# One copy of the bias table, four product banks, and a lane for the compression in a two-layer hybrid-attention trunk

## The chip, the cores and the metric

The kernel runs on one NeuronCore of a Trainium2 chip. The metric is the time of one execution on the device in microseconds, the median of several runs; lower is better. A profile of one execution shows, for each engine, which instruction ran when. TensorE (PE) multiplies, with its weight loads shown apart (PEld); VectorE (DVE) and ScalarE (ACT) work element by element; GpSimd (POOL) does little here but issues some of the DMAs; SyncE (SP) issues the others.

## The reference

A trunk of two layers works on a sequence of 256 rows of width 1024 in float32. Each layer has a gated FFN, three kinds of attention side by side whose outputs are gated and merged, a second gated FFN, and a gated addition of a per-layer embedding:

```python
for i in range(DEPTH):
    h = h + 0.5 * swiglu(rms_norm(h, norm_g[i, 0]), ffn1_wi[i], ffn1_wo[i])
    n = rms_norm(h, norm_g[i, 1])
    (aq, ak, av, bq, bkc, ..., ga, gb, gc) = split_cols(n @ w_in[i], IN_SPLITS)
    ya = diff_attention(aq, ak, av, bias_a, lam, ...)         # A: two softmaxes, subtracted
    yb = nsa_attention(bq, compress(bkc), compress(bvc), bks, bvs, bkw, bvw, ...)  # B
    yc = swa_sink_attention(cq, ck, cv, bias_c, sinks[i])     # C: window 128, with a sink
    merged = sigmoid(ga) * (ya @ w_branch[i, 0]) + sigmoid(gb) * (yb @ w_branch[i, 1]) \
           + sigmoid(gc) * (yc @ w_branch[i, 2])
    h = h + merged @ w_out[i]
    h = h + 0.5 * swiglu(rms_norm(h, norm_g[i, 2]), ffn2_wi[i], ffn2_wo[i])
    h = h + sigmoid(rms_norm(h, norm_g[i, 3]) @ w_ple_gate[i]) * (p[i] @ w_ple[i])
return rms_norm(h, final_norm)
```

All three attentions add to their scores a bias that depends on the head (20 of them) and on the distance between query and key alone. In attention B the keys and values are also compressed: blocks of 32 rows, one every 16, pass through a small network with GELU (`w1`, then `w2`) to 15 compressed keys and values, to which every query attends as well.

## The kernel before

**Products.** The 256 rows are two tiles of 128, called t = 0 and 1. Each product has a weight stream: pieces of 128 x 1024 floats (512 KB) come in by DMA to one of four `raw` buffers (L257, issued on SP), and each is split into a rounded part `wh` (ScalarE, L213) and a remainder `wl` (VectorE, L208). `mul3` (L219) makes one full-precision product out of three fast matmuls, L220 to L222. `product` (L290) walks over the k chunks of tile 0, then of tile 1, and calls `done(t, ps)` when a tile's sum is complete. `done` reads the PSUM bank and frees it. Products take their bank from `mm_bank` (L191), which has two; two more banks (tag "s") hold attention's scores, three (tag "tp") transposes, one (tag "y") attention outputs.

**Order.** The program is written in one order, and a scheduler places each engine's instructions by when their inputs are ready, earlier-written ones first. After that each engine runs its list strictly in order. A DMA's wait holds back what is behind it on its queue.

**FFN.** `ffn` (L437) runs 11 products `ff` of 512 columns (gate and up halves of 256), whose `done` is `gated` (L452): ScalarE's `act` (L458), then VectorE's multiplication (L459). Their results are transposed by DMA (`turn_by_dma`, L420). The two output products are `fo`.

**Attention beside products.** Attention A, C and B are generators. `Flow` (L153) holds one of them at a time and advances it by `pace` steps on each k step of a product (`tick`); `join` (L171) runs the rest of it in one go. L955 to L977 give the order: A runs beside the products Ck, Cq and Bk and is joined; C runs beside Bv, Bq and branch 0 and is joined; B runs beside the product of the compression, branch 2 and the gates of branch 1, and is joined before the last two branch products (L941).

**Compression.** `compress` (L685) multiplies with `w1` (L701 to L707), copies the sum (L709), folds it (`gl`, L712), goes through GELU, multiplies with `w2` for keys (`kc`) and, group by group, for values (`vc`, 16 rows, L735 to L740), all in one stretch. `attend_cmp` (L761) scores against the compressed keys and turns the eight heads' probabilities by eight transposes of 16 columns each (`pct`, L787), into `pcT` with 16 rows. The last step of each group and tile of B multiplies `pcT` with `vc` (L843) and gathers the output (L748).

**Bias.** `setup` (L1041), run between products of the first FFN, makes a table of 20 heads x 384 distances, writes it to DRAM (`table`, 30 KB, L1061), and has POOL copy it 128 times into `rev` (3840 KB, L1062). A band of four heads for 128 queries x 256 keys is then one DMA that steps one element back per partition (`rev_band`, L1033): two for `cbias` in `setup`, and five in each layer's attention. `softmax` (L523) adds the band to the scores and takes the minimum in one VectorE instruction (L529).

Of the kernel before, what the change touches and what calls it, by code (L numbers as in the profile page):

```python
# [26 lines left out]
NB = 20  # L27
# [6 lines left out]
PACE_A, PACE_B, PACE_C = 0.75, 0.7, 0.6  # L34
# [101 lines left out]
def _constants():  # L136
    u = np.arange(REV)
    dist = 255 - u
# [10 lines left out]
    return {"onehot": onehot, "dead": dead, "cmask": cmask, "ident": np.eye(128, dtype=np.float32),  # L149
# [3 lines left out]
class Flow:  # L153


    def __init__(self):
        self.side, self.pace, self.due = None, 0.0, 0.0

    def start(self, side, pace):
        self.side, self.pace, self.due = side, pace, 0.0  # L160

    def tick(self):
        if self.side is not None:
            self.due += self.pace
            while self.due >= 1.0:
                self.due -= 1.0
                if next(self.side, self) is self:
                    self.side = None
                    return

    def join(self):  # L171
        if self.side is not None:
            for _ in self.side:
                pass
            self.side = None
# [3 lines left out]
def trunk(ctx: ExitStack, tc: tile.TileContext, a: dict, out: bass.AP, index: list):  # L179
# [11 lines left out]
    def mm_bank(name):  # L191
        return bank("mm", 2, name)

# [96 lines left out]
    def product(lhs, nk, done, name, w, skew=SKEW):  # L290

        def run():
            ps = [None] * NT
            for step in range(nk + skew):
                for t, k in ((0, step), (1, step - skew)):
                    if 0 <= k < nk:
                        wh, wl = w(k)
                        if k == 0:
                            ps[t] = mm_bank(f"{name}{t}")
                        xh, xl = lhs(t, k)  # L300
                        mul3(ps[t][:, :w.width], xh, xl, wh, wl, k == 0, k == nk - 1)
                        if k == nk - 1:
                            done(t, ps[t])
# [184 lines left out]
    def attention(i, norm, after):  # L488
# [3 lines left out]
        def begin():  # L492
            nonlocal pool
            pool = phase("attn")
            for t in range(NT):
                merged[t] = pool.tile([128, D], F32, name=f"merged{t}")
# [58 lines left out]
        def band(first):  # L555
            b = pool.tile([128, 4, 256], F32, tag="band", bufs=2, name="band")
            rev_band(b, first)
# [23 lines left out]
        def attend_a():  # L581
            bnd = band(0)

            def first(u):
# [6 lines left out]
                for st in softmax([p[:, j, :nk] for j in range(4)], [s[j // 2][:, j % 2, :nk] for j in range(4)],  # L591
                                  [bnd[:, 2 * m + j % 2, 256 - nk:] for j in range(4)]):
# [90 lines left out]
        kc, vc = [None], [None]  # L683

        def compress():  # L685
# [22 lines left out]
            c_sb = stage()  # L708
            nc.vector.tensor_copy(c_sb[:64], c_ps[:64])  # L709
            g_ps = tp_bank("gl")[:, :128]  # L710
            for k in range(4):
                nc.tensor.matmul(g_ps[:, 32 * k:32 * k + 32], c_sb[:64, 128 * k:128 * k + 128], fold, start=True, stop=True)  # L712
# [3 lines left out]
            nc.vector.tensor_tensor(gl, gl, g_ps, op=ALU.mult)  # L716
            nc.scalar.activation(gl, gl, AF.Tanh, scale=math.sqrt(2.0 / math.pi))
            nc.vector.tensor_scalar(gl, gl, 0.5, 0.5, op0=ALU.mult, op1=ALU.add)
            nc.vector.tensor_tensor(gl, gl, g_ps, op=ALU.mult)
            hid = pool.tile([128, 2, 128], F32R, name="hid")  # L720
            split(hid[:, 0], hid[:, 1], gl)
            w2h, w2l = w2(0)
# [10 lines left out]
            split(kt[:, 0], kt[:, 1], kbd)  # L733
            v_ps = tp_bank("vc")
# [4 lines left out]
            vc[0] = pool.tile([16, 2, 128], F32R, name="vc")  # L739
            values(vc[0], v_ps[:16, :128], None)  # L740
# [20 lines left out]
        def attend_cmp(t):  # L761
# [20 lines left out]
            for g in range(2):  # L782
                ps = tp_bank("pct")
                for par in range(2):
                    for m in range(2):
                        j = 2 * par + m
                        nc.tensor.transpose(ps[:16, 128 * j:128 * j + 128], p[:, 4 * g + 2 * m + par, :], ident)  # L787
                T = pool.tile([16, 2, 512], F32R, tag="pcT", bufs=2, name="pcT")
                split(T[:, 0], T[:, 1], ps[:16])
                pcT[t, g] = T  # L790
# [381 lines left out]
```

## Time and profile before

| | us |
|---|---|
| median of 3 runs | 1372.09 (1371.64 to 1373.06) |
| the profiled execution | 1372.78 |
| its span, first to last instruction | 1371.0 |
| TensorE busy | 1341.5 |
| VectorE busy | 944.7 |
| ScalarE busy | 779.4 |
| chain that ended last: TensorE / DMA / VectorE / ScalarE | 88% / 5% / 3% / 2% |

The busy time of TensorE is modelled from the ends of pipelined matmuls, which overlap, so counts of matmuls in a window tell more than its busy share. "Granted clock" is the share of TensorE's full 2.4 GHz that it was given; 0.50 is 1.2 GHz.

### The profile page before, as it was taken

Reading aid. Unit: us, or ns where it says so; the run is one execution under the profiler, and the core shown is the slowest. Engines: PE = TensorE matmul, PEld = TensorE weight load, DVE = VectorE, ACT = ScalarE, POOL = GpSimd, SP = SyncE. Lnnn points to the kernel's source line nnn. Section 1 sums busy time; section 2 is a strip of 40 time slices with the busy share of each in tenths; the row PEclk is TensorE's granted clock in tenths of the full one; section 3 lists DMA queues with packets and bytes.
Section 4 is the critical chain, followed back from the end, with each engine's and each line's share of the span. In section 5 each row is a group of like instructions: output and inputs, shape, how many; then the busy total and the mean of one; then the engine's idle time right before and its main releaser. Section 6 shows DMA issues by size and latency. Waiting matters only on the chain.

```text
span 1371.0 us, 18293 instructions
## 1 busy us (share of the span) xinstructions
PE 1341.5 (98%) x6454; PEld 1098.2 (80%) x6454; DVE 944.7 (69%) x1779; ACT 779.4 (57%) x1378; POOL 19.0 (1%) x37
## 2 busy tenths in 40 slices
PE   8988999999999999999999999999999999999997
PEld 6766888887787788888888888888887778888886
DVE  7546656777886766766677665667697776776665
ACT  7435445668766455545665444566785656455454
POOL 0000000000000000000000000000000000000000
PEclk9999999999999999999999999999999999999999
DMA  8797757444653467775657885754547435777662
GB/s 306 199 265 227 216 177 237 142 152 156 215 175 109 153 189 213 215 210 192 203 189 219 223 226 171 235 170 137 162 151 232 127 122 168 216 222 218 194 202 84
DMA packets 121993, 261.07 MB, mean 190 GB/s; under 512 B 56816, under 2 KB 62372, under 8 KB 121774
## 3 DMA queue, kind: packets, MB, share of 16 engines
q1 hardware_dynamic: 121006, 254.34, 60.3%
q0 software_dynamic: 464, 5.01, 1.2%
q8 instruction: 50, 0.82, 0.2%
q10 hardware_dynamic: 432, 0.56, 0.1%
q14 instruction: 41, 0.34, 0.1%
HBM read 247.26 MB, written 5.01 MB: 184 GB/s over the span
## 4 chain that ended last, share of the span: by engine, by line
PE 88%; DMA 5%; DVE 3%; ACT 2%; issue 1%; SPq 0%; POOLq 0%; POOL 0%; DVEq 0%; ACTq 0%
PE ff L220 10%; PE ff L221 10%; PE ff L222 10%; PE fo L221 6%; PE fo L220 6%; PE fo L222 6%; DMA raw<-in_wst 4%; PE gate L220 3%; PE gate L221 3%; PE gate L222 3%; PE s L520 2%; PE A L220 2%; PE A L222 2%; PE A L221 2%; PE br L220 2%; PE br L222 2%
## 5 line engine op out<-in xcount | busy, mean ns | idle before, releaser
L208 DVE TENSOR_TENSOR wl<-raw,wh 128x1024 fp32r<-128x1024 f32 (+1 forms) x450 | 540.8, 1211 | 176.2 <-ACT wh L213 169.5
L213 ACT ACTIVATE wh<-raw 128x1024 fp32r<-128x1024 f32 (+1 forms) x450 | 469.4, 1049 | 227.7 <-PE fo L222 85.8
L220 PE MATMUL ff<-wh,nT 128*128 128x512 f32 x704 | 276.8, 395 | 13.0 <-DVE gated L459 8.4
L221 PE MATMUL ff<-wl,nT 128*128 128x512 f32 x704 | 276.2, 393 | 0.7 <-DVE wl L208 0.5
L222 PE MATMUL ff<-wh,nT 128*128 128x512 f32 x704 | 275.0, 391 | 0.0
L220 PEld LDWEIGHTS ff<-wh,nT 128*128 128x128 f32 x704 | 133.2, 189 | 45.6 <-DVE gated L459 11.0
L221 PEld LDWEIGHTS ff<-wl,nT 128*128 128x128 f32 x704 | 133.3, 189 | 30.0 <-DVE wl L208 2.7
L222 PEld LDWEIGHTS ff<-wh,nT 128*128 128x128 f32 x704 | 133.3, 189 | 27.9
L221 PE MATMUL fo<-wl,gT 128*128 128x512 f32 x352 | 134.2, 392 | 0.0
L222 PE MATMUL fo<-wh,gT 128*128 128x512 f32 x352 | 133.7, 389 | 0.0
L220 PE MATMUL fo<-wh,gT 128*128 128x512 f32 x352 | 133.2, 390 | 0.0
L458 ACT ACTIVATE act<-ff,stats 128x256 f32<-128x256 f32 x88 | 41.4, 473 | 104.0 <-PE ff L222 103.9
L459 DVE TENSOR_TENSOR gated<-act,ff 128x256 f32<-128x256 f32 x88 | 36.6, 417 | 74.3 <-ACT act L458 74.3
L221 PE MATMUL gate<-wl,nT 128*128 128x512 f32 x192 | 77.5, 404 | 1.5 <-DVE wl L208 1.5
L220 PE MATMUL gate<-wh,nT 128*128 128x512 f32 x192 | 78.8, 410 | 0.0
L222 PE MATMUL gate<-wh,nT 128*128 128x512 f32 x192 | 77.3, 402 | 0.0
L220 PEld LDWEIGHTS fo<-wh,gT 128*128 128x128 f32 x352 | 66.1, 188 | 13.9
L222 PEld LDWEIGHTS fo<-wh,gT 128*128 128x128 f32 x352 | 66.1, 188 | 13.4
L221 PEld LDWEIGHTS fo<-wl,gT 128*128 128x128 f32 x352 | 66.1, 188 | 13.3
L213 ACT ACTIVATE gT<-whole 128x512 fp32r<-128x512 f32 (+1 forms) x48 | 28.3, 590 | 63.0 <-DVE whole L432 62.2
L531 ACT ACTIVATE p<-p,st 128x128 f32<-128x128 f32 (+1 forms) x128 | 56.8, 447 | 12.2 <-DVE st L529 12.0
L320 ACT ACTIVATE nT<-nt,ngt 128x128 fp32r<-128x128 f32 x112 | 32.0, 369 | 30.8 <-PE nt L228 30.8
(297 smaller groups left out, 2002.8 us busy)
## 6 DMA issues: line engine op xcount, KB each, us to landing
raw<-in_wst SPq DMA_DIRECT2D x438, 512.0 KB, 4.4
band<-rev SPq DMA_DIRECT2D x10, 512.0 KB, 4.1
rev<-table POOLq DMA_DIRECT2D x1, 3840.0 KB, 18.3
raw<-in_wbv SPq DMA_DIRECT2D x4, 420.0 KB, 3.0
flip<-cut SPq DMA_TRANSPOSE x96, 3.8
xt<-in_xt SPq DMA_DIRECT2D x4, 256.0 KB, 5.3
raw<-in_wst SPq DMA_DIRECT2D x4, 256.0 KB, 4.0
h<-in_x SPq DMA_DIRECT2D x2, 512.0 KB, 8.0
```

What stands on the lines that cost most here:

```text
L208: nc.vector.tensor_tensor(o, x, y, op=ALU.subtract)
L213: nc.scalar.activation(hi, src, AF.Copy)
L220: nc.tensor.matmul(ps, xh, wh, start=start, stop=False)
L221: nc.tensor.matmul(ps, xh, wl, start=False, stop=False)
L222: nc.tensor.matmul(ps, xl, wh, start=False, stop=stop)
L320: ins = nc.scalar.activation(T[:, 0, k + m, :], src[:, 128 * m:128 * m + 128], AF.Copy, scale=ngt[:, self.row, k + m:k + m + 1])
L458: nc.scalar.activation(act, ps[:, :256], AF.Silu, scale=norm.r(t))
L459: nc.vector.tensor_tensor(held[t][:, 256 * (f % 2):256 * (f % 2) + 256], act, ps[:, 256:], op=ALU.mult)
L520: nc.tensor.matmul(o, q[r, x, qb[m], t * 128:(t + 1) * 128], kk, start=x + y == 0, stop=x == 1)
L531: nc.scalar.activation(p[j], p[j], AF.Exp, bias=st[:, j:j + 1], scale=-1.0, accum_out=st[:, n + j:n + j + 1])
```

## The change

- The table is stored in ascending distance, and the 128 copies (`rev`) are gone. A band is read straight from the table, one element forward per partition (`read_band`), and holds its keys in reverse; every reader goes over it backwards, with step -1 or -16 (`back`).
- `product` takes its bank from `product_bank`: outside attention from four banks in turn, `mm` twice, then `s` twice; in attention from `mm`'s two.
- `product` calls `done` under a priority that ranks its instructions as if they had been written 150 instructions earlier.
- `Flow` has lanes. Each lane is a list of generators, run one after the other, so C follows A and B follows C without a join; a join is now asked for where a branch needs its input. B's pace goes from 0.7 to 0.75.
- What follows the `w1` product in `compress` is a generator of its own, `compressed`, in lane 1 at pace 1. `w2` is fetched by itself ahead of the compression instead of in the weight stream. Attention B takes up the compressed keys at the end of its last step for a tile, instead of before its first one.
- Compressed values are made for all eight heads at once with 128 rows (`rows_`), and the probabilities of a tile are turned by one transpose. For each group a mask (`hmask`, a new constant) keeps that group's heads (`own`), and the result is split then.

```diff
-PACE_A, PACE_B, PACE_C = 0.75, 0.7, 0.6
+PACE_A, PACE_B, PACE_C = 0.75, 0.75, 0.6
...
-    dist = 255 - u
+    dist = u - 127
...
+    def start(self, side, pace, lane=0):
+        self.lanes.setdefault(lane, [[], 0.0])[0].append((side, pace))
+        return side
...
+    def join(self, side):
+        while any(s is side for lane in self.lanes.values() for s, _ in lane[0]):
+            for lane in self.lanes.values():
+                if lane[0]:
+                    self.step(lane)
...
+    wide = [True, 0]
+    def product_bank(name):
+        wide[1] += 1
+        return bank("s" if wide[0] and wide[1] % 4 >= 2 else "mm", 2, name)
...
-                            ps[t] = mm_bank(f"{name}{t}")
+                            ps[t] = product_bank(f"{name}{t}")
...
-                            done(t, ps[t])
+                            with tc.high_priority(offset=150):
+                                done(t, ps[t])
...
-                                  [bnd[:, 2 * m + j % 2, 256 - nk:] for j in range(4)]):
+                                  [back(bnd[:, 2 * m + j % 2], nk) for j in range(4)]):
...
+        def second_weights():
+            nonlocal w2
+            raw = base.tile([128, SUB], F32, tag="raw", bufs=RAWS, name="w2raw")
+            nc.sync.dma_start(raw[:, :384], a["w2"][i])
+            w2 = pool.tile([128, 2, 384], F32R, name="w2")
+            split(w2[:, 0], w2[:, 1], raw[:, :384])
...
-            for g in range(2):
-                for f in range(2):
-                    s, n = slice(256 + 64 * f, 320 + 64 * f), slice(64 + 32 * f + 16 * g, 80 + 32 * f + 16 * g)
-                    mul3(v_ps[:16, 64 * g:64 * g + 64], hid[:, 0, n], hid[:, 1, n], w2h[:, s], w2l[:, s], f == 0, f == 1)
+            rows_ = base.tile([128, 2, 2, 128], F32R, tag="stage", bufs=4, name="rows")
+            for f in range(2):
+                for x in range(2):
+                    nc.vector.tensor_copy(rows_[:, x, f]..., hid[:, x, 64 + 32 * f:96 + 32 * f]...)
+            for f in range(2):
+                s = slice(256 + 64 * f, 320 + 64 * f)
+                mul3(v_ps[:, :64], rows_[:, 0, f], rows_[:, 1, f], w2h[:, s], w2l[:, s], f == 0, f == 1)
...
-            for g in range(2):
-                ps = tp_bank("pct")
-                for par in range(2):
-                    for m in range(2):
-                        j = 2 * par + m
-                        nc.tensor.transpose(ps[:16, 128 * j:128 * j + 128], p[:, 4 * g + 2 * m + par, :], ident)
-                T = pool.tile([16, 2, 512], F32R, tag="pcT", bufs=2, name="pcT")
-                split(T[:, 0], T[:, 1], ps[:16])
+            ps = tp_bank("pct")
+            transposes(ps, [p.rearrange("p h n -> p (h n)")])
+            pcT[t] = pool.tile([128, 128], F32, tag="pcT", bufs=2, name="pcT")
+            nc.scalar.activation(pcT[t], ps[:, :128], AF.Copy)
...
+        def own(t, g):
+            o = stage("own").rearrange("p (j q) -> p j q", j=4)
+            nc.vector.tensor_tensor(o, pcT[t][:, None, :].to_broadcast([128, 4, 128]),
+                                    hmask[:, 4 * g:4 * g + 4, None].to_broadcast([128, 4, 128]), op=ALU.mult)
+            T = pool.tile([128, 2, 4, 128], F32R, tag="pT", bufs=3, name="pcT")
+            split(T[:, 0], T[:, 1], o)
+            return T
...
-                    weighted(y_ps[g, t], vc[0][:, g], pcT[t, g], False, True)
+                    if t not in pcT:
+                        while kc[0] is None:
+                            yield
+                        yield from attend_cmp(t)
+                    T = own(t, g)
+                    yield
+                    weighted(y_ps[g, t], vc[0][:, 0], T.rearrange("p x j q -> p x (j q)"), False, True)
...
-        yield flow.join
-        yield lambda: flow.start(attend_c(), PACE_C)
+        yield lambda: start("c", attend_c(), PACE_C)
...
-        yield flow.join
-        yield lambda: flow.start(attend_b(), PACE_B)
+        yield second_weights
+        yield lambda: start("b", attend_b(), PACE_B)
...
         yield compress
+        yield lambda: start("compressed", compressed(), 1.0, 1)
...
-    def rev_band(b, first, queue=nc.sync):
-        ap = rev[:, :]
-        queue.dma_start(b, bass.AP(tensor=ap.tensor, offset=ap.offset + first * REV + 127,
-                                   ap=[[NB * REV - 1, 128], [REV, 4], [1, 256]]))
+    def read_band(b, first, queue=nc.sync):
+        ap = table[:, :]
+        queue.dma_start(b, bass.AP(tensor=ap.tensor, offset=ap.offset + first * REV, ap=[[1, 128], [REV, 4], [1, 256]]))
+    def back(b, n, step=1):
+        return bass.AP(tensor=b.tensor, offset=b.offset + step * (n - 1), ap=list(b.ap)[:-1] + [[-step, n]])
...
-        nc.gpsimd.dma_start(rev, table.to_broadcast([128, NB * REV]))
```

## Rows read from the trace of the kernel before

**Rows 1.** The page: busy us, share of the span, instructions of each engine.
```profile
PE 1341.5 (98%) x6454; PEld 1098.2 (80%) x6454; DVE 944.7 (69%) x1779; ACT 779.4 (57%) x1378; POOL 19.0 (1%) x37
```

**Rows 2.** TensorE's waits: who <- whom: us in total, times, longest us.
```profile
PE ff L220 <- DVE gated L459: 8.4, 5, 3.2
...
PE gl L712 <- DVE stage L709: 1.8, 2, 1.0
PE pt L228 <- DVE half L655: 1.6, 2, 0.8
PE gate L221 <- DVE wl L208: 1.5, 2, 0.8
...
PE br L220 <- ACT yB L213: 0.4, 2, 0.2
```

**Rows 3.** Windows: stretch, length, each engine's busy us (instructions), clock, DMA share, GB/s.
```profile
30.00:40.00 10.00, 7.60 (x27) 5.85 (x26) 6.88 (x12) 3.39 (x6) 0.00 (x0) 0.83 0.85 227
80.00:120.00 40.00, 30.55 (x114) 22.57 (x114) 21.23 (x29) 15.32 (x19) 1.54 (x2) 0.91 0.95 267
130.00:140.00 10.00, 10.00 (x46) 8.29 (x45) 6.23 (x10) 5.09 (x6) 0.00 (x0) 1.00 0.65 209
```

**Rows 4.** Timeline around 30: start, us, engine, line, what, count, [idle before <- releaser].
```profile
32.91 0.80 PE L220 MATMUL ff<-wh,nT 128*128 128x512 f32 x1 [2.40 <-DVE gated L459]
30.06 2.47 DVE L208 TENSOR_TENSOR wl<-raw,wh 128x1024 fp32r<-128x1024 f32 x2 [0.70 <-ACT wh L213]
32.44 0.75 DVE L459 TENSOR_TENSOR gated<-act,ff 128x256 f32<-128x256 f32 x2
```

**Rows 5.** The broadcast: POOL's timeline; DMA queues and issues in 74:86; TensorE's timeline.
```profile
71.47 0.56 POOL L1062 DMA_DIRECT2D rev<-table  x1 [1.51 <-DMA table<-tb]
...
q0 software_dynamic: 115, 3.44, 82.0%
q1 hardware_dynamic: 101, 0.41, 12.2%
raw<-in_wst SPq DMA_DIRECT2D x1, 512.0 KB, 17.4
...
91.07 1.22 PE L220 MATMUL ff<-wh,nT 128*128 128x512 f32 x2 [3.37 <-ACT wh L213]
```

**Rows 6.** DMA queues, issues in 92:101 (packets, MB, share; landing us); the page's bands.
```profile
q0 software_dynamic: 285, 1.04, 59.2%
...
raw<-in_wst SPq DMA_DIRECT2D x4, 512.0 KB, 12.1
...
band<-rev SPq DMA_DIRECT2D x10, 512.0 KB, 4.1
```

**Rows 7.** TensorE's timeline: compressed probabilities turned, multiplied, and the compressed values.
```profile
396.80 1.03 PE L787 MATMUL pct<-ident,pc 128*16 128x128 f32 x8
...
441.60 0.49 PE L745 MATMUL yb<-pcT,vc 16*128 16x512 f32 x1
441.93 0.39 PE L746 MATMUL yb<-pcT,vc 16*128 16x512 f32 x1
...
378.67 0.19 PE L221 MATMUL vc<-wl,hid 128*16 128x64 f32 x1
378.70 0.19 PE L222 MATMUL vc<-wh,hid 128*16 128x64 f32 x1
```

**Rows 8.** Windows at half clock in attention (columns as in the third group).
```profile
411.75:415.17 3.42, 3.42 (x9) 2.74 (x9) 2.78 (x14) 2.53 (x10) 0.00 (x0) 0.50 0.48 153
1036.39:1039.81 3.42, 3.42 (x10) 2.63 (x9) 2.75 (x5) 0.58 (x3) 0.00 (x0) 0.50 0.85 253
```

**Rows 9.** VectorE: groups (count | busy us, mean ns | idle), line 692, a window of attention.
```profile
324.00:456.00 132.00, 130.22 (x695) 104.81 (x695) 107.74 (x256) 87.62 (x188) 0.00 (x0) 0.99 0.51 165
L529 DVE CUSTOM_DVE_ANT_0 p<-s,band 128x256 f32<-128x256 f32 x48 | 17.6, 419 | 7.9 <-PE pt L228 7.9
L692 DVE TENSOR_TENSOR e<-half,pos x8: 625/641/658, 329.2 to 997.9; 128x256 f32<-128x256 f32 x4, 128x248 f32<-128x248 f32 x4
```

More of the change, by code (lines that the diff above doesn't have):

```diff
@@ L148, in _constants @@
     cmask = ((128 * t + ql - 16 * m - 31 >= 0) & (m < 15)).astype(np.float32).reshape(128, 32)
-    return {"onehot": onehot, "dead": dead, "cmask": cmask, "ident": np.eye(128, dtype=np.float32),
+    own = np.arange(8)[:, None] == np.array([4 * g + 2 * pr + par for g in range(2) for par in range(2) for pr in range(2)])
+    hmask = own.repeat(16, 0).astype(np.float32)
+    return {"onehot": onehot, "dead": dead, "cmask": cmask, "hmask": hmask, "ident": np.eye(128, dtype=np.float32),
             "fold": np.tile(np.eye(32, dtype=np.float32), (2, 1))}
@@ L156, in __init__, with step @@
     def __init__(self):
-        self.side, self.pace, self.due = None, 0.0, 0.0
-    def start(self, side, pace):
-        self.side, self.pace, self.due = side, pace, 0.0
-    def tick(self):
[L163 to L175, printed above, removed]
+        self.lanes = {}
+    def start(self, side, pace, lane=0):
+        self.lanes.setdefault(lane, [[], 0.0])[0].append((side, pace))
+        return side
+    def step(self, lane):
+        if next(lane[0][0][0], self) is self:
+            lane[0].pop(0)
+    def tick(self):
+        for lane in self.lanes.values():
+            if lane[0]:
+                lane[1] += lane[0][0][1]
+                while lane[1] >= 1.0 and lane[0]:
+                    lane[1] -= 1.0
+                    self.step(lane)
+    def join(self, side):
+        while any(s is side for lane in self.lanes.values() for s, _ in lane[0]):
+            for lane in self.lanes.values():
+                if lane[0]:
+                    self.step(lane)
 @with_exitstack
@@ L494, in begin @@
             pool = phase("attn")
+            wide[0] = False
             for t in range(NT):
@@ L805, in first @@
                     sr = [s[j // 2].rearrange("p m (k n) -> p m k n", k=2)[:, j % 2, k] for j, k in rows]
-                    br = [bnd[g][:, j, 128:] for j, k in rows]
+                    br = [back(bnd[g][:, j], 128) for j, k in rows]
                 else:
@@ L811, in first @@
                     sr = [s[j // 2][:, j % 2] for j in range(4)]
-                    br = [bnd[g][:, j] for j in range(4)]
+                    br = [back(bnd[g][:, j], 256) for j in range(4)]
                 n = len(pr)
@@ L879, in first @@
                 st = None
-                for st in softmax(pr, [s[j // 2][:, j % 2, :nk] for j in range(4)], [bnd[g][:, j, 256 - nk:] for j in range(4)], sink):
+                for st in softmax(pr, [s[j // 2][:, j % 2, :nk] for j in range(4)], [back(bnd[g][:, j], nk) for j in range(4)], sink):
                     yield
@@ L902, in attend_c, with branch @@
             yield from pipelined([(g, t) for g in range(2) for t in range(NT)], first, second)
-        def branch(b, yT, last=False):
+        def branch(b, yT, side, last=False):
             def parts(c):
@@ L946, in branch @@
                     yield gated(c, both[c][0])
+                    if c == 0:
+                        yield lambda: flow.join(sides[side])
                     yield mixed(c, both[c][1])
@@ L957, in attention, with start @@
         yield project("A2", done_av)
-        yield lambda: flow.start(attend_a(), PACE_A)
+        sides = {}
+        def start(name, side, pace, lane=0):
+            sides[name] = flow.start(side, pace, lane)
+        yield lambda: start("a", attend_a(), PACE_A)
         yield project("Ck", done_ck, 256)
@@ L967, in attention @@
         yield project("Bq", done_q(qB, "qB"))
-        yield from branch(0, yA)
-        yield flow.join
-        yield lambda: flow.start(attend_b(), PACE_B)
+        yield from branch(0, yA, "a")
+        yield second_weights
+        yield lambda: start("b", attend_b(), PACE_B)
         w1 = streamed(i, "w1", 256)
-        w2 = Weights(384, [(a["w2"][i], 384)], 1)
         yield compress
-        yield from branch(2, yC)
-        yield from branch(1, yB, True)
+        yield lambda: start("compressed", compressed(), 1.0, 1)
+        yield from branch(2, yC, "c")
+        yield from branch(1, yB, "b", True)
+        yield lambda: wide.__setitem__(0, True)
         for c in range(2):
@@ L1022, in trunk @@
     cmask = base.tile([128, 2, 16], F32, name="cmask")
+    hmask = base.tile([128, 8], F32, name="hmask")
     nsink = base.tile([128, DEPTH, 8], F32, name="nsink")
```

44 lines of the change are left out of this document (27 added, 17 removed).

## Prediction

> **What bounds the kernel now.** I read the page's busy times first: TensorE is busy 1341.5 of 1371.0 us [rows 1], so only work taken off TensorE, or one of its waits, can move the end; VectorE at 69% matters only where it is locally full. Then the list of what TensorE waited for [rows 2]: barely 20 us, of which 8.4 are waits of the first product's matmuls on the VectorE instruction `gated` (L459), which frees their PSUM bank. Then the windows [rows 3], to see what a wait really costs. An undisturbed window of 10 us holds 46 matmuls, two of them cut by its edges, so 44 per 10 us or 0.227 us each: the busy time of 0.39 us that the profile gives one matmul overlaps the next, so I count matmuls and not busy time. 30:40 holds 27, so (46-27) x 0.227 = 4.3 us are lost there. 80:120 holds 114 where 176+2 would stand: 64 x 0.227 = 14.5 us. Together 18.8 us in the first FFN, more than the listed waits, because the granted clock falls to 1.2 GHz after each long wait (mean 0.83 and 0.91 of 2.4 GHz in those windows).
>
> **Part 1, the broadcast to `rev` goes.** POOL issues it at 71.47 [rows 5]. In 74:86 the software queue took 82.0% of the DMA engines' time and the weights' queue 12.2%, 0.41 MB in 12 us, where one weight piece is 0.5 MB; a piece issued there landed after 17.4 us. TensorE lived on what was stored until 91.07 - 3.37 = 87.70 and then stood, and the later waits in 80:120 are the recovery. What is late next are the two band reads that POOL issues behind it (1.04 MB, 59.2% of 9 us = 5.3 us of all the engines), which now come right behind the table's write. Weights that were in flight with them landed after a median of 12.1 us [rows 6]. TensorE stood only 87.70 - 71.47 = 16.2 us after the broadcast had begun, so 12.1 us plus one split pair of some 2.3 us still fits. I take the whole **-14.5 us**; bounds -14.5 and -7.5 (5.3 us of DMA time plus one clock fall of 1.7 given back).
>
> The bands themselves now all come from one row of 30 KB instead of 128 copies, so they could read slower than 4.1 us [rows 6]. The broadcast read that same 30 KB 128 times at 3.44 MB in 12 us, 287 GB/s [rows 5], which is 1.8 us for a band; I price the reads at nothing, with a bound of one band's time, 4.1 us, where attention first needs one.
> The Trainium skill, "DMA: Bandwidth & Descriptors", section "Latency and other measured facts", speaks against this: it gives 103 GB/s instead of 207 where per-partition streams run at a bad row pitch, and infers that they meet on one HBM channel. Streams that start 4 bytes apart would be the extreme of that; at 103 GB/s a band would take 5.1 us, 1.0 more than now. The trace's 287 GB/s speaks against it, and the sum does not use it.
>
> **Part 2, four banks outside attention.** At 30:40 the third product needs a bank that `gated` frees at 32.44 + 0.75, behind two weight splits of later pieces [rows 4]. With four banks TensorE goes on into a bank freed a product earlier, and the weights it needs had been split before. **-4.3 us**; bound 0, if weights turn out to be the later of the two. The other waits on `gated` lie in 80:120, where they are counted already, or ahead of it, where I leave them at 0.
>
> **Part 3, compression's values.** Of 32 `pct` transposes 4 remain; eight take 1.03 us, about 0.11 us apart when the last one's own length is left out [rows 7]: 28 x 0.11 = -3.1. The 16 matmuls on `pcT` with 16 rows start 0.33 us apart against 0.227 for the same 512 columns with 128 rows: -1.6. The `vc` matmuls go from 24 at a pace of 0.03 to 12 with a full-width weight load; taking the `pct` pace, +0.6. All of it is TensorE time in stretches where TensorE never rests: **-4.1 us**.
> VectorE pays: eight masked copies (`own`) and eight `rows_` copies, of at most 512 columns. L208 needs 2.47 / 2 = 1.23 us for 1024 [rows 4], so an estimate of 0.62 for 512, at most 16 x 0.62 = 10 us in all, 5 per layer. In 324:456 VectorE is busy 107.74 of 132 [rows 9], so 5 fits in the 24 that are free; price 0, bound +5 per layer.
>
> **Part 4, the compression in a lane and no joins.** The wait of `gl` for its copy (1.8 us for both layers, [rows 2]) goes, since eight `gl` matmuls no longer follow the copy at once: -1.8. The join after Bk drained six leftover steps of attention A in one burst, where `pt` waited 1.6 us for a bank held by `half` [rows 2]; counting steps, all six now fall into Bv: -1.6. `w2` leaves the weights' queue, where it stood ahead of branch 2's first gate piece; of the 1.5 us that the gates waited on `wl` [rows 2] I take half, -0.8. What is late next there is VectorE, which has the steps of attention B. The clock fall at 1036.39 [rows 8] follows the `gl` wait of layer 1; with it, half of 3.42 us: -1.7 (bound 0). The fall at 411.75, and its twin in layer 1, follow no wait; I leave them.
> In the other direction: the last product with `vc` now has a mask multiply (0.62 us) and a split pair before it instead of a ready tile, and the gather, and behind it yB and the last branch product, wait for it. TensorE already waits 0.4 us there [rows 2]. Fully on the path it is about 2 us per layer, fully beside the other transposes 0; I take 0.7: +1.4. By counting, B has 4 steps left at its join instead of 2, and attention B passes 14 empty steps instead of 8. **Part 4: -4.5 us.**
>
> **Part 5, backward bias reads.** 128 bias instructions (L529) read one operand with step -1; the trace has no negative step. The nearest are L529 itself (0.419 us for 256 columns) and L692, whose strided operand makes 256 columns last 0.641 [rows 9]. The low end is 0 (a gain is excluded: nothing else in the instruction shrinks). The high end is 0.22 us for each of 64 wide and 0.15 for each of 64 narrow ones, 24 us of VectorE over both layers. I take 0, as L529 keeps its length, operand type and order of work.
> [...] The sum uses the rows' two ends.
>
> **Part 6, 150 instructions ahead.** Evacuations, their transposes and the FFN's DMA transposes pass weight splits on ScalarE and VectorE and weight loads on SP. With a TensorE wait on `wl` of at most 0.8 us anywhere [rows 2], the splits have lead; price 0. One more small constant (`hmask`) on SP: 0.
>
> **Sum.** -14.5 - 4.3 - 4.1 - 4.5 = -27.4. The profiled execution took 1372.78, 0.7 above the median of the runs (1372.09), so 1345.4 in its terms, about **1345** as a median.
>
> **Rivals.**
> (a) *The bands take the broadcast's place.* They collide with the weights right behind the table, at the same spot. For it: 59.2% of the engines in 92:101. Against: 12.1 us of landing is inside the 16 us. Price 7: 1352.
> (b) *VectorE becomes the bound in attention*, by backward reads and `own` together. The two ends of its load are 24 + 10 us, and VectorE has 24 us free in 324:456 alone. If a third of it reaches TensorE, 12: 1357; all of it would be 1379.
> (c) *Slower: what is put ahead starves the weight splits.* The two layers have 104 products and 208 evacuations. If an evacuation on VectorE displaces the next piece's `wl`, TensorE waits as it does once at each branch 2 gate, 1.5 / 2 = 0.75 us [rows 2]. From 27.4 / 0.75 = 37 of the 208, every sixth, the gain is gone; at one in three it is 52 - 27 = 25 us slower, 1397. Against it: the splits' lead over the first FFN's 16 us without weights.
> (d) *More than forecast*: the two clock falls without a wait go too (-3.4), and the tail of `own` is free (-1.4), the remaining `wl` wait as well (-0.8): 1339.
> (e) *It does nothing measurable*: the lost time returns as other waits piece by piece, 1372.
>
> **How the numbers follow.** Forecast (1341 to 1350) 0.57, (a) 0.12, (b) 0.12, (c) 0.05, (d) 0.11, (e) 0.03. The range 1335 to 1360 takes in (d), (a) and most of (b), and leaves out (c), (e) and the worst of (b), together under 2 in 10. No change means within 0.2%, 2.7 us, about what a measurement can tell: faster 0.92, same 0.03, slower 0.05.
>
> **What would show it.** Right: 80:120 holds some 176 matmuls at clock 1.00, no `gated` wait at 30, 4 `pct` transposes and no `gl` wait. Wrong: raw pieces still landing after 15 us around 75; L529 longer than 0.45 us at 256 columns; TensorE waits on `wl` at product boundaries; new clock falls in 320:450 and its twin; a longer wait before the last branch product.

## The result and the profile after

The changed kernel takes **1357.01 us** (median of 4 runs, 1356.52 to 1358.54) where the kernel before took 1371.87 in the same session: ratio 0.9895, 95% interval 0.9878 to 0.9912, a gain of 14.9 us. 27.4 had been forecast, a time of 1345. The time lies in the range and on the side that was given; the gain is a little over half of the one worked out. The profiled execution took 1356.52 us, its span is 1354.7.

The page of the changed kernel (busy us, share of the span, instructions), beside [rows 1]:

```profile
PE 1331.4 (98%) x6414; PEld 1096.5 (81%) x6414; DVE 947.4 (70%) x1795; ACT 782.2 (58%) x1382; POOL 18.5 (1%) x36
...
band<-table SPq DMA_DIRECT2D x10, 512.0 KB, 4.9
```

TensorE still fills 98% of the span. Its waits in the changed kernel, beside [rows 2] (who <- whom: us in total, times, longest us):

```profile
PE pct L243 <- DVE pc L822: 6.2, 2, 3.3
PE ff L236 <- DVE wl L223: 1.9, 2, 1.7
PE pt L243 <- DVE pT L223: 1.9, 2, 0.9
...
PE mt L243 <- DVE merged L969: 1.3, 2, 0.6
PE yb L787 <- DVE yt L797: 0.6, 2, 0.5
```

The waits on `gated`, `gl`, `half` and on the gates' `wl` are gone. A wait of about 3 us in each layer has come: `pct`, the transpose of compression's probabilities, waits for the last VectorE step on them. Windows of the changed kernel (stretch, length, each engine's busy us and instructions, granted clock, DMA share, GB/s), beside [rows 3]:

```profile
30.00:40.00 10.00, 10.00 (x45) 8.27 (x45) 7.07 (x14) 4.26 (x7) 0.00 (x0) 1.00 1.02 270
64.00:66.00 2.00, 1.11 (x5) 0.57 (x4) 1.29 (x3) 0.38 (x2) 0.00 (x0) 1.00 0.91 292
80.00:120.00 40.00, 40.00 (x178) 33.14 (x177) 27.99 (x40) 21.26 (x27) 1.63 (x2) 1.00 0.80 232
...
413.00:432.00 19.00, 13.99 (x73) 10.24 (x73) 17.57 (x45) 12.21 (x30) 0.00 (x0) 1.00 0.28 87
1080.00:1100.00 20.00, 15.54 (x73) 12.43 (x72) 17.59 (x45) 12.13 (x29) 0.00 (x0) 0.83 0.33 102
```

In the first FFN the two stretches that the prediction named are whole: 45 matmuls in 30:40 instead of 27, 178 in 80:120 instead of 114, both at 2.4 GHz. What is new stands in the last two rows, the end of attention in either layer: TensorE is idle 19 - 13.99 = 5.0 us and 20 - 15.54 = 4.5 us. In the kernel before, the end of layer 0's attention had almost no idle time:

```profile
440.00:460.00 20.00, 19.79 (x94) 15.02 (x93) 16.55 (x24) 11.13 (x18) 0.00 (x0) 1.00 0.45 141
```

In layer 1 of the changed kernel the clock falls there too: a mean of 0.83 over 20 us is some 6.8 us at 1.2 GHz, part of it idle. VectorE is busy 17.57 of 19 us in layer 0's window.

**Where the time went**, read from the first and last start of one tile's matmuls (min/median/max ns, then first and last start). The kernel before, layer 0:

```profile
L220 PE MATMUL A<-wh,nT x48: 389/389/484, 209.6 to 244.0; 128*128 128x512 f32 x48
...
L222 PE MATMUL gate<-wh,nT x96: 388/389/628, 307.4 to 443.6; 128*128 128x512 f32 x96
...
L746 PE MATMUL yb<-pcT,vc x4: 392/392/392, 409.6 to 453.4; 16*128 16x512 f32 x4
...
L222 PE MATMUL wo<-wh,mT x32: 389/389/397, 459.5 to 483.9; 128*128 128x512 f32 x32
```

The changed kernel:

```profile
L235 PE MATMUL A<-wh,nT x48: 387/389/477, 191.7 to 226.1; 128*128 128x512 f32 x48
...
L237 PE MATMUL gate<-wh,nT x96: 387/389/499, 285.8 to 413.0; 128*128 128x512 f32 x96
...
L788 PE MATMUL yb<-pcT,vc x4: 389/394/496, 409.4 to 437.9; 128*128 128x512 f32 x4
...
L237 PE MATMUL wo<-wh,mT x32: 387/389/476, 435.8 to 467.1; 128*128 128x512 f32 x32
```

Attention begins 209.6 - 191.7 = 17.9 us earlier: all of the gain. Its last gate product starts 443.6 - 413.0 = 30.6 us earlier, 12.7 more; but attention B's last output product (`yb`) comes only 15.5 earlier and the last product of the output projection (`wo`) 16.8. Attention as a whole, `A` to `wo`, takes 275.4 us instead of 274.3; in layer 1 276.5 instead of 275.9. So two layers that were to gain 8.6 us (parts 3 and 4) lost 1.7.

### The profile page after: what moved, and what is told of

It reads as the page before. It is cut to its first block, busy times and chain, and to the rows that moved or that the text cites. A ratio compares the mean times of both kernels' runs of the same rounds, so it can differ in the third digit from the quotient of the medians.

```text
span 1354.7 us, 18246 instructions
## 1 busy us (share of the span) xinstructions
PE 1331.4 (98%) x6414; PEld 1096.5 (81%) x6414; DVE 947.4 (70%) x1795; ACT 782.2 (58%) x1382; POOL 18.5 (1%) x36
## 4 chain that ended last, share of the span: by engine, by line
PE 92%; DVE 3%; DMA 2%; ACT 2%; issue 1%; SPq 0%; POOLq 0%; POOL 0%; DVEq 0%; ACTq 0%
PE ff L236 11%; PE ff L237 11%; PE ff L235 11%; PE fo L236 6%; PE fo L235 6%; PE fo L237 6%; PE gate L235 3%; PE gate L237 3%; PE gate L236 3%; PE s L537 3%; PE A L236 2%; PE A L235 2%; PE A L237 2%; PE br L236 1%; PE br L235 1%; PE br L237 1%
## 5 line engine op out<-in xcount | busy, mean ns | idle before, releaser
L237 PE MATMUL ff<-wh,nT 128*128 128x512 f32 x704 | 273.4, 390 | 0.0
L235 PE MATMUL ff<-wh,nT 128*128 128x512 f32 x704 | 270.8, 391 | 0.0
L235 PE MATMUL gate<-wh,nT 128*128 128x512 f32 x192 | 77.0, 403 | 0.0
L237 PE MATMUL gate<-wh,nT 128*128 128x512 f32 x192 | 75.8, 395 | 0.0
L448 DVE COPY whole<-flip 128x512 uint16<-128x512 uint16 (+1 forms) x96 | 38.2, 434 | 12.8 <-DMA flip<-cut 12.2
```

The costliest lines, as they stand in the source:

```text
L235: nc.tensor.matmul(ps, xh, wh, start=start, stop=False)
L237: nc.tensor.matmul(ps, xl, wh, start=False, stop=stop)
L448: tc.keep_in_program_order(nc.vector.tensor_copy(halves(whole)[:, :128 * m, w], flip[:, w, :m].rearrange("p a b -> p (a b)")))
```

## The experiments

The theories, as they are named in the expectations. L and P (in the first four), S and K each name one cause of the new wait: L the place at which compression's scores are asked for, P what is scheduled ahead, S the empty steps that attention B takes in the program text, K compression's own latency and the PSUM bank held for it. O says that the wait follows from the order in which B's instructions stand against the gates'. V says that B's end is set elsewhere, so that whatever is gained ahead of it is lost there.

**Compression's scores for tile 1 asked for early.**

```diff
                 if yB[t] is None:
                     yB[t] = y_tile("yB")
+                    if t == 1:
+                        yield from attend_cmp(t)
```

> The changed kernel, but the compressed probabilities of tile 1 are computed at the start of attention B's first step for that tile, as before the change, instead of at its end. Theory L (late chain): TensorE's waits ahead of the last branch product (about 5.5 us in layer 0 and 8 to 10 in layer 1, clock fall included) come from that chain standing at the end of attention B; they shrink to 1 or 2 us a layer and the time falls by 8 to 11, to 1346 to 1349. Theory P (the 150 instructions ahead hold attention B back): the chain is only the place where it shows, another step of B becomes the last, and the time stays within 1354 to 1358.

1355.25 us, ratio 0.9877 (0.9860 to 0.9893). Its waits:

```profile
PE yb L788 <- DVE pT L223: 3.8, 2, 1.9
PE br L235 <- ACT yB L228: 2.9, 2, 1.5
PE ff L236 <- DVE wl L223: 2.7, 2, 2.4
```

The `pct` wait is gone, and other steps of B are waited for instead: `pT` for 3.8 us and `yB` for 2.9, both layers together. Attention takes 274.7 and 276.2 us in the two layers, against 275.4 and 276.5. L falls as the cause: taking the wait away doesn't take the time away.

**Nothing scheduled ahead.**

```diff
-                            with tc.high_priority(offset=150):
-                                done(t, ps[t])
+                            done(t, ps[t])
```

> The changed kernel, but what follows a product keeps its own place in the order instead of 150 instructions ahead. Theory P: attention B is no longer passed by the branches' work on VectorE, the waits before the last branch product shrink and the time falls to 1346 to 1350. Theory L: those waits stay, 1354 to 1360. If the rank itself gained something in the FFNs, slower than 1357.

1360.7 us, 0.9916 (0.9901 to 0.9930), 3.7 above the changed kernel. `pct` waits 6.3 us as before, so P falls. And `half` waits again:

```profile
PE pct L243 <- DVE pc L821: 6.3, 2, 3.2
PE mt L243 <- DVE merged L968: 3.4, 2, 2.7
PE gate L236 <- DVE wl L223: 2.4, 2, 1.2
PE pt L243 <- DVE half L671: 2.1, 2, 1.0
```

The prediction gave the end of that wait to the join that was taken out after Bk, and half of the gates' wait for `wl` to the earlier `w2`; both waits are here, with the join gone and `w2` earlier, and both are gone in a kernel further down that has scheduling ahead without these two. They end by scheduling ahead.

**Two banks everywhere.**

```diff
-        return bank("s" if wide[0] and wide[1] % 4 >= 2 else "mm", 2, name)
+        return bank("mm", 2, name)
```

> The changed kernel, but products take their bank from the two of before everywhere. By the sum of the prediction the wait at 30 us comes back with its clock fall: 4.3 us slower than the change, 1361. If the 150 instructions ahead alone free the banks in time, no difference: 1357.

1364.95 us, 0.9950 (0.9936 to 0.9965): 7.9 above the changed kernel, where 4.3 was forecast for the banks. The window that they repair:

```profile
30.00:40.00 10.00, 6.94 (x24) 5.22 (x23) 7.48 (x12) 3.73 (x5) 0.00 (x0) 0.83 0.89 246
```

Attention begins 5.3 us later (197.0 against 191.7), and it is 3.1 us longer in layer 0 and 1.0 in layer 1. The output projection no longer starts beside B's end: its first product comes at 450.1 instead of 431.9, and TensorE waits 1.5 us for `yB` ahead of it, where the changed kernel waits 0.2. Not all of the 3.1 belongs to that: in this execution the clock fell twice in layer 0's attention, for 3.4 us each, and in the changed kernel's not at all.

**The single table alone** (the kernel before, with `read_band` and `back`; the rest as it was).

```diff
-        nc.gpsimd.dma_start(rev, table.to_broadcast([128, NB * REV]))
...
-                                  [bnd[:, 2 * m + j % 2, 256 - nk:] for j in range(4)]):
+                                  [back(bnd[:, 2 * m + j % 2], nk) for j in range(4)]):
```

> The kernel before, with the single table and the backward reads alone. By the prediction the stretch 80 to 120 us fills up and nothing else changes: 14.5 us less than before, 1357 to 1358, with the wait at 30 us still there. If the waits of that stretch belonged to the two banks rather than to the broadcast: 1365 to 1370. If backward reads cost VectorE anything, the bias instruction is longer than 0.42 us for 256 columns and the time is above 1360.

1359.13 us, 0.9908 (0.9893 to 0.9922): -12.6, most of what the whole change brings. The windows (30:40 as before, 80:120 whole):

```profile
30.00:40.00 10.00, 6.56 (x22) 4.98 (x21) 6.52 (x11) 3.81 (x6) 0.00 (x0) 0.83 0.84 233
80.00:120.00 40.00, 40.00 (x178) 33.15 (x177) 28.99 (x42) 20.89 (x27) 0.00 (x0) 1.00 0.93 259
```

**Compression's networks in one piece, and in a faster lane; attention B at a faster pace; the last two together.**

```diff
-        yield lambda: start("compressed", compressed(), 1.0, 1)
+        yield lambda: list(compressed())
```

```diff
-        yield lambda: start("compressed", compressed(), 1.0, 1)
+        yield lambda: start("compressed", compressed(), 2.0, 1)
```

```diff
-PACE_A, PACE_B, PACE_C = 0.75, 0.75, 0.6
+PACE_A, PACE_B, PACE_C = 0.75, 0.9, 0.6
```

> The changed kernel with compression's networks issued at once behind compress, in one piece, instead of one piece per tick in a lane of their own; nothing else is undone. Theory S (steps lost): attention B's first output unit needs compression's values; while they are not there, each tick that falls to B is spent on an empty step. Counted through the loops, the changed kernel loses 14 of B's steps that way and has 4 steps left at the join ahead of the last branch products; with the networks in one piece it loses 6 and has none left. The changed kernel's wait of some 6 us per layer ahead of the last branch product then goes, the wait for gl returns (1.9 us in the kernel before, both layers together): 1357 - 12 + 2 = 1347, range 1345 to 1351, no pct wait above 1 us, and the last branch product starts 5 to 7 us earlier in both layers. Theory V (the end of attention B is set by VectorE's work, not by where B's steps stand): the tail moves by less than 2 us per layer and the time stays at 1355 to 1359. Theory K (it is compression's own latency, 52 us from its last product to the first transposed values): kc and pct come 10 us earlier or more, and the time is as in S; S and K are told apart by the next two kernels.

> The changed kernel with compression's lane at two pieces per tick instead of one. Theory S: B loses 9 or 10 steps instead of 14 and has none left at the join; the tail's wait goes as with the networks in one piece, and gl is still covered by a product's matmuls: 1345 to 1350. If the pieces now come faster than VectorE and ScalarE can serve them, TensorE waits at gl, kc or vc, up to 2 us a layer, which takes the time to 1350 or 1351. Theory V: 1355 to 1359.

> The changed kernel with attention B's pace at 0.9 steps per tick instead of 0.75, compression's lane as it is. Theory S: B loses more empty steps (19 by the count) but catches up afterwards, and has none left at the join: the tail's wait goes although compression's values come no earlier, 1345 to 1351. Theory K: the values come as late as in the changed kernel (first pct at 395 to 397 us), so the tail keeps its wait and the time stays within 1354 to 1359. Theory V: VectorE, 80 to 90 per cent busy beside the gates of the last branch, can't follow the faster steps, TensorE waits for pT or pc ahead of the gates' end, and the time is 1355 to 1362.

> Both: compression's lane at two pieces per tick and attention B at 0.9 steps per tick. Theory S: B is done some 11 ticks ahead of the join, with nothing gained beyond the kernel with two pieces per tick, because the tail is gone there already: 1345 to 1351, within 2 us of it. Theory V: slower than with the faster lane alone, by the waits for VectorE that the denser steps bring, 1352 to 1360.

In one piece: 1358.6 us, 0.9906 (0.9889 to 0.9922). Faster lane: 1358.78, 0.9905 (0.9888 to 0.9922). Faster pace: 1355.32, 0.9885 (0.9867 to 0.9903). Both: 1357.48, 0.9901 (0.9880 to 0.9923). None of the four comes near the 1345 to 1351 of S, and for a plain reason: the builder sorts the instructions into the engines' queues by its own estimate of when each can run, and it undid the edits. S's count of steps in the program's text therefore says nothing of the chip. The queues of the first two are those of the changed kernel, instruction for instruction on every engine; the last differs from it in up to 8 lines an engine. Only the pace alone moved more, in layer 1, and not the time. So a place in the program text is no place in time here, and these kernels say nothing on K. They do say how far medians of one program lie apart: 1357.0, 1358.6, 1358.8. Less than 2 us is not read from here on. The same holds for a single trace: layer 0 of the faster pace has the changed kernel's order but for a few neighbours that swap places, and its attention takes 277.6 us instead of 275.4, since the clock fell there in that execution.

**What the parts are worth in the order of the kernel before.** The single table and four banks, without lane, values and scheduling ahead; then the same with scheduling ahead.

```diff
-                            ps[t] = mm_bank(f"{name}{t}")
+                            ps[t] = product_bank(f"{name}{t}")
...
-                            done(t, ps[t])
+                            with tc.high_priority(offset=150):
+                                done(t, ps[t])
```

The last three lines are in the second kernel only.

> The kernel before with the single table read backward and the four banks; no lane, no new form of compression's values, nothing scheduled ahead. Theory O (the order of attention B's end is what costs): the attention block keeps the order it has in the kernel before, where the last branch product is ready when B is, so the whole worth of the banks shows: 1359.1 (the table alone) less 5 in the first feed-forward and 2 to 3 by the output projection that can start beside B's tail, less 2 for clock falls that go with the wait at 30: 1349 to 1353, faster than the changed kernel by 4 or more; no pct wait above 1 us. Theory V (attention B ends where VectorE lets it, so every microsecond gained ahead of it is lost at its end): 1355 to 1358.

> The same with what follows a product scheduled 150 instructions ahead: the changed kernel without the lane, without the new form of compression's values and without the moved joins. Theory O with the lane and the values to blame: the 3.7 us of the changed kernel's scheduling ahead come on top: 1346 to 1350. If it is scheduling ahead that lets the gates run away from attention B (their end 30 us earlier instead of 20), the pct or another wait of 2 to 3 us a layer ahead of the last branch product is here too and the time is 1353 to 1358, no better than without it.

1357.00 us, 0.9900 (0.9871 to 0.9929), and 1360.98, 0.9929 (0.9904 to 0.9954). O's first number, 1349 to 1353, isn't met: the time is that of the changed kernel, though no `pct` wait shows. The second kernel lies above both of its numbers. With the changed kernel and the one with nothing ahead this makes a square; all four have the table and the banks:

| | nothing ahead | 150 ahead |
|---|---|---|
| compression as before | 1357.0 | 1361.0 |
| compression reworked, lane, moved joins | 1360.7 | 1357.0 |

By the medians, scheduling ahead alone costs 4 us, the rework alone costs 3.7, and together they cost nothing. By the ratios, each against the kernel before in its own session, it is 4.0, 2.2 and nothing, and the intervals of neighbours overlap. The length of attention in the traces points the same way: 275.0 and 274.3 us in the two layers with neither, 277.7 and 277.4 with scheduling ahead, 279.6 and 277.4 with the rework, 275.4 and 276.5 with both. But each is one execution, and executions of one order differ by some 2 us. So that the two parts make up for each other's cost is likely, and the size of the costs stays open. Scheduling ahead alone has a new wait of its own, and none on `gl`, `half` or the gates' `wl`:

```profile
PE mt L235 <- DVE merged L929: 5.7, 2, 2.8
PE yb L755 <- DVE pT L215: 2.5, 2, 1.3
```

**Compression ahead of branch 0.**

```diff
+        w1 = streamed(i, "w1", 256)
+        yield second_weights
+        yield compress
+        yield lambda: start("compressed", compressed(), 1.0, 1)
         yield from branch(0, yA, "a")
-        yield second_weights
         yield lambda: start("b", attend_b(), PACE_B)
-        w1 = streamed(i, "w1", 256)
-        yield compress
-        yield lambda: start("compressed", compressed(), 1.0, 1)
```

> The changed kernel with compression's products and networks moved ahead of branch 0 (some 35 us of TensorE's work earlier), so that its values are there before attention B's first output unit wants them and the one bank for B's outputs isn't held for them. Theory K (that bank, held from 358 to 406 us, delays all of B): B's outputs end 10 us earlier or more and the wait ahead of the last branch product goes: 1345 to 1350. Theory V: B's end does not move by more than 2 us and neither does the time: 1355 to 1359, with another wait in place of pct's.

1379.45 us, 1.0056 (1.0033 to 1.0079), slower than the kernel before. Compression's products began 21 us earlier (311.2 against 332.6) and B ended 8 us later after attention's start, where K wanted it 10 us earlier. The stretch ahead of them, which has gate matmuls in the changed kernel, was left without gates (columns as in the windows above):

```profile
290.00:311.00 21.00, 20.09 (x87) 16.88 (x87) 14.42 (x59) 16.63 (x58) 0.69 (x1) 0.51 0.23 78
969.00:993.00 24.00, 23.00 (x96) 19.41 (x97) 17.42 (x76) 17.89 (x65) 0.69 (x1) 0.51 0.26 90
```

TensorE ran at 1.2 GHz for 20 us in layer 0 and 24 in layer 1, from 0.6 us after a wait of 1.7 us for attention A's turned probabilities; another of 0.9 us follows within it. Half of the 20 us is lost work, some 10 us of the 10.9 by which layer 0's attention is longer than in the changed kernel. Without them B would end only about 2 us earlier than in the changed kernel, so K falls in this form even so.

**Attention B's steps scheduled ahead too**, with the early scores of the first experiment.

```diff
-        yield lambda: start("b", attend_b(), PACE_B)
+        yield lambda: start("b", ahead(attend_b(), 100), PACE_B)
```

`ahead` runs each step of B under `tc.high_priority(offset=100)`.

> The changed kernel with attention B's own steps scheduled 100 instructions ahead as well, and compression's scores for the second tile asked for at that tile's first output step. In the instruction queues as built, B's last scores of compression then stand before the end of the last gates on TensorE, and the gates end some 3 us of matmuls later than in the changed kernel, so that they cover more of B's end. Theory O (the order that the scheduler gives attention B against the gates sets the wait): the pct wait goes, TensorE's idle time behind the last gate falls from 6 to under 3 us a layer, 1349 to 1353. Theory V (B's end follows from the length of its own chain of VectorE and ScalarE steps, and every order loses at the end what it gained before): another step of B is waited for instead, the attention block still takes 274 to 278 us from its first product to its last, 1354 to 1359.

1360.62 us, 0.9912 (0.9892 to 0.9932). The order did change: the gates end 7 us later after attention's start, compression's last scores come 18 us earlier, no clock falls, and `pct` isn't waited for. O expected 1349 to 1353, V 1354 to 1359 and 274 to 278 us of attention; attention takes 277.4 and 277.2 us, and four other steps took the place of `pct`:

```profile
PE br L235 <- ACT yB L228: 2.9, 2, 1.5
PE gate L235 <- ACT wh L228: 2.9, 2, 1.6
PE pt L243 <- DVE p L876: 1.9, 2, 1.0
PE yb L788 <- DVE pT L223: 1.8, 2, 0.9
```

**One number under all of them.** Layer 0, us after the first matmul of `A`, from lines like those of the first section:

| kernel | last gate | B's last output | TensorE busy up to there | last `wo` |
|---|---|---|---|---|
| before | 234.0 | 243.8 | 241.2 | 274.3 |
| table alone | 235.6 | 245.4 | 242.6 | 275.9 |
| table, banks | 235.5 | 242.6 | 239.9 | 275.0 |
| table, banks, ahead | 224.8 | 245.6 | 243.7 | 277.7 |
| changed | 221.3 | 246.2 | 241.2 | 275.4 |
| changed, not ahead | 225.5 | 247.8 | 239.9 | 279.6 |
| changed, two banks | 221.4 | 245.6 | 241.2 | 278.5 |
| changed, faster pace | 221.3 | 248.4 | 244.3 | 277.6 |
| changed, early scores | 223.2 | 244.1 | 241.3 | 274.7 |
| changed, B ahead | 228.0 | 246.8 | 242.8 | 277.4 |
| changed, compression first | 236.5 | 254.1 | 248.8 | 286.3 |

The last gate moves by 15 us, and with one exception B's last output stays between 242.6 and 248.4. V says that whatever is gained ahead of B's end is lost there, and by and large that is so in these kernels. What sets B's end is another question, and the fourth column gives a plain part of the answer:

```profile
209.60:453.40 243.80, 241.18 (x1324) 197.82 (x1323) 184.66 (x439) 160.68 (x356) 3.34 (x5) 0.99 0.52 168
191.70:437.90 246.20, 241.19 (x1313) 198.42 (x1312) 186.90 (x448) 162.05 (x358) 3.33 (x5) 1.00 0.50 166
```

The first row is the kernel before, the second the changed one, each from the first matmul of `A` to B's last output. TensorE is busy for 241.2 us in both, in the kernel before with 3.4 us of it at 1.2 GHz. Behind B's last output stand only the end of the last branch product, the output projection and a few transposes, some 30 us, so nearly all the rest of attention's matmuls come before it in every order. Doing the gates earlier only changes what they are done beside. What an order can win or lose at B's end is TensorE's idle time ahead of it, 2.6 us in the kernel before and 5.0 in the changed one, and what a low clock costs, as in the exception. So TensorE's own work accounts for nearly all of the time to B's end. Why some 5 us of idle time remain there in the changed kernel is not shown: that B's chain of transposes, splits and softmax steps is too long for what can stand beside it fits, but no run shortened that chain by itself.

## Why the prediction came out as it did

**Part 1** (-14.5) held: -12.6 alone, 178 matmuls in 80:120 at full clock. The bands didn't take the broadcast's place: rival (a) didn't come. They do read slower from one row, 4.9 us against 4.1 [rows 6], and nothing waits for them. The Trainium skill, "DMA: Bandwidth & Descriptors", section "Latency and other measured facts", had by its lower rate, 103 GB/s, 5.1 us as an estimate; the trace lies nearer to that than to the 1.8 that the prediction worked out from the broadcast, and no run shows why.

**Part 2** (-4.3) was right in its mechanism and place: parts 1 and 2 together bring attention 17.9 us forward where 18.8 were forecast. Beside the missing 0.9 stands a new wait for `wl` of 1.7 us in the first FFN (0.9 of it in the window 64:66); that TensorE, some 4 us earlier, now catches up with its weights is a reading, not shown. The banks' second use, output projection beside B's end, wasn't seen. By the medians the banks are worth 7.9 us in the changed kernel, but only about 2 in the order of the kernel before.

**Part 3** (-4.1) is the first step that failed. The rows are gone: `pct` has 2 transposes a layer instead of 16, and by the time from each matmul's start to the next that is 1.5 us a layer, as forecast. The products on `pcT` gave 0.25 us a layer instead of 0.8. The error is the sentence that all of it was TensorE time where TensorE never rests. At the end of attention it now rests, and just this step is what it rests for. And as much as `pct` gave went to attention's scores: their 168 matmuls a layer take 16.3 us in the kernel before and 17.8 in the changed one. With nothing scheduled ahead they take 15.4, so it is the order and not the new form; what in the order makes them dearer is not shown.

**Part 4** (-4.5) is the second. The waits it named did go: `gl`, `half` and the gates' `wl`, and the clock fall behind `gl`. Two of them, `half` and `wl`, went by part 6 and not by the lane. But the term against it, +1.4 for B's end in both layers, is the one that was mis-sized: it measured 5.0 and 4.5 us of idle TensorE, and 6.8 us at 1.2 GHz in layer 1. The timeline of the changed kernel shows why "4 steps left instead of 2" was no measure (start, us, what, [idle before <- releaser]):

```profile
417.14 0.66 PE L243 MATMUL pt<-ident,p 128*128 128x128 f32 x4 [0.94 <-DVE pT L223]
...
422.25 0.50 PE L788 MATMUL yb<-pT,vB 128*128 128x512 f32 x1
425.57 0.33 PE L243 MATMUL pct<-ident,pc 128*128 128x128 f32 x1 [2.81 <-DVE pc L822]
425.73 1.47 PE L243 MATMUL pt<-ident,p 128*128 128x128 f32 x12
427.65 0.50 PE L787 MATMUL yb<-pcT,vc 128*128 128x512 f32 x1 [0.45 <-ACT pcT L228]
```

The last gate started at 413.0. What is left of B's second tile from here on are transposes, scores and output products that each need VectorE or ScalarE first, and no gate is left to put between them. In the kernel before the gates ran until 443.6, beside these same steps. The steps were counted in the program's text, which isn't the order on the chip. And to free TensorE ahead of the gates' end was worth nothing: it let the gates be done earlier, not B. Over the whole of layer 0's attention TensorE is busy 1.9 us less than before, 269.7 instead of 271.6, and idle 3.0 us more, 6.1 instead of 3.1.

**Part 5** (0, up to 24 us) was right. The bias instruction at 256 columns:

```profile
L546 DVE CUSTOM_DVE_ANT_0 p<-s,band 128x256 f32<-128x256 f32 x48 | 17.6, 419 | 2.2 <-PE pt L243 2.2
```

419 ns read backward, 419 before [rows 9]. So rival (b) gave the right time, 1357, by luck: of its 34 us of VectorE load the 24 for backward reads aren't there. What it had right is that VectorE is nearly full where the time is lost, 17.57 of 19 us. That the time lies inside the range is luck in the same way: it missed the forecast's 1341 to 1350, and the range went up to 1360 to take in most of (b).

**Part 6** (0) was wrong as a separate term: by the medians 4 us dearer alone, 3.7 cheaper with the rework. Its reason held, the weight splits aren't starved. What it moves is the order of B against the gates, and it ends the waits on `half` and the gates' `wl`. Rival (c) does not show: the only wait on `wl` of any size is that one in the first FFN.

Of what was to show the prediction wrong, two came: the longer wait ahead of the last branch product, and new clock falls at layer 1's twin of that place. Of the 12.5 us missed, 0.9 are in parts 1 and 2, and 5.4 and 4.9 in the two attention blocks; the rest is the distance of the two profiled executions from their medians. By the medians no kernel of the study beats the changed one by more than 2 us; the table and the banks alone reach its time.

## What to carry to other kernels

A gain on the busiest engine is only worth what is left of it at the next point where that engine must wait for a chain of others; look there first, and ask what will cover that chain once the filling work is done earlier. Where a builder sorts the queues, read the order from the queues and not from the program, and measure parts both alone and left out, since here two of them seem to cost 2 to 4 us each and nothing together. When a point doesn't move whatever is done ahead of it, first add up how much of the busiest engine's own work stands ahead of it. The simplest part, reading one 30 KB table backward instead of writing 128 copies of it, was most of the gain: 12.6 us by itself.

## What was not expected of the hardware

A step of -1 costs VectorE nothing in the bias instruction: 419 ns at 256 columns both ways, and 286 both ways at 128. With the DRAM-to-DRAM broadcast out of the way, weights in 74:86 land in 4.8 us where a piece took 17.4 [rows 5]. And what follows a short gap can differ much: with compression ahead of branch 0, TensorE ran at 1.2 GHz for 20 us behind a wait of 1.7 us, while after the 2.8 us wait for `pct` in the changed kernel's layer 0 its clock didn't fall at all (in another execution of the same queues it fell there for 3.4 us). What kept the clock low for 20 us no run shows.
